# A hybrid decoder trunk on one core: the mixer's weight scan with three buffers, the gate product on GpSimd, and layer 1's FFN groups and small sums in another order

## The chip, the cores and the metric

The kernel runs on one core of a Trainium2 chip. The metric is the time of one execution on the device in microseconds (us); a kernel is given by the median of its runs. The engines work at the same time, each through its own list of instructions in order: TensorE (PE in the profile; PEld is its weight load), VectorE (DVE), ScalarE (ACT), GpSimd (POOL) and SyncE (SP, which issues DMA transfers here). An instruction can wait for another engine's result; everything behind it on its own engine then waits too. L12 is line 12 of the kernel.

## What is computed

Two layers on 1024 tokens of width 1024, float32 in and out. Layer 0 mixes by differential attention and a Mamba-2 state-space part, layer 1 by a Conformer convolution module; each is followed by a gated FFN with a causal convolution of width 3 over the tokens.

```python
def conformer_conv(h, ...):                      # layer 1's mixer
    u = h @ pw1_w + pw1_b
    u = u[..., :1024] * sigmoid(u[..., 1024:])
    u = causal_dwconv(u, dw_w, dw_b)             # width 31
    u = silu(layer_norm(u, ln_w, ln_b))
    return u @ pw2_w + pw2_b

def conv_ffn(h, up_w, conv_w, conv_b, down_w):
    u = causal_dwconv(h @ up_w, conv_w, conv_b)  # width 3
    gate, val = u[..., :2816], u[..., 2816:]
    return (silu(gate) * val) @ down_w

def reference(x, ...):
    for i in range(2):
        if i == 0:
            x = x + hybrid_mixer(rms_norm(x, mix_norm_w), ...)
        else:
            x = x + conformer_conv(rms_norm(x, conf_norm_w), ...)
        x = x + conv_ffn(rms_norm(x, ffn_norm_w[i]), ...)
    return x
```

## The kernel before

**Tiles.** Tokens lie along the free dimension, in two halves of 512 (`h` = 0, 1). A product of the trunk is `gemm`: for each of 8 blocks of 128 channels three matmuls of 128x512 float16, since both sides are split into a high and a low part; so 24 matmuls, all on L239. The FFN's 2816 columns are 22 tiles ("pairs", a gate tile and a value tile). They stand in groups: one of 6 pairs that is computed for both halves with its weights loaded once (`BOTH`; A in layer 0, E in layer 1), and B and C of 8 pairs each, computed for one half at a time (`HALVES`; B[0], B[1] and so on). `ups` makes a group's pairs, `close` scales and splits its gated values to float16 (L935 on ScalarE, L936 on VectorE), `down` multiplies by the down weights and adds into x (L1063).

**Weights.** `loads` brings a weight tile by SyncE's queue into one of three raw buffers. ScalarE casts it (L94, or L98), and the low part comes from GpSimd (L95, L96; for the "pool" groups and the conv weights) or VectorE (L99). Pool groups are those of the half whose conv runs at the time: layer 0's B, C of half 1, layer 1's of half 0.

**Powers.** The scale of a weight matrix is a power of two, found from the sum of squares over the whole matrix. `scan` makes it in the background: it loads a piece by ScalarE's own queue, squares and sums it there (L147). In the mixer it goes over layer 0's up weights, 88 pieces of 256 KB, with one buffer, a step each time that `mix` has made a step of the mixer's own work. `root` and `total` turn sums into a power: a reduction (L132), one small matmul that sums over partitions (L110), and small VectorE operations (L112, L120, L125, L126). `powers(1)` does so for layer 1's up weights and its norm weight.

**Norms.** `rms`: token sums of squares by small matmuls (L903), an inverse root by VectorE (L248 to L254), a broadcast by matmul into PSUM (L259), then for each block a product on VectorE (L920), a cast on ScalarE (L932) and a subtraction on VectorE (L933). `ln` does it twice: the mean (L903, L259; subtracted in L1144, squared on ScalarE, summed in L1150), then the variance (L903, L259), then L1158, a SiLU, and the split.

**Order.** Each engine's order follows from the order in which the program records its instructions, with priorities (`high_priority`) that let weight loads and evictions go ahead. Generators yield where other work may be put between. `along` runs the conv (`p1`, `ln`: 30 multiply-adds of 128x512 a block on VectorE, L1123) beside FFN pairs of the other half. `weave` runs a norm beside products. In layer 1: conv of half 1 with B[0] and C[0] beside it; then `p2(1)`, the conv module's second product; then the norm of half 1 woven with what is left of B[0] and C[0] (`f`); then B[1], C[1] and last E for both halves.

**The gate.** For a pair, `conv3` evicts the product with the width-3 convolution (ScalarE L945 or L947, VectorE L951), ScalarE applies the SiLU (L981), `gate` multiplies the two (L961 on VectorE) and ScalarE squares the result for its power (L962). These tiles are `a`, with six buffers.

Of the kernel before, what the change touches and what calls it, by code (L numbers as in the profile page):

```python
# [20 lines left out]
P = 128  # L21
# [19 lines left out]
MIXER = {"raw": 2, "whl": 4, "g": 10, "scan": 1, "sums": 1}  # L41
PIECE = 4, 8
TRUNK = {"raw": 3, "w": 4, "g": 20, "sv": 1, "hf": 2, "scan": 2, "gm": 4, "gs": 4, "sums": 5}


class Net:
# [91 lines left out]
    def scan(self, name, srcs, depth):  # L138
# [5 lines left out]
        for i, src in enumerate(srcs + [None] * depth):  # L144
# [3 lines left out]
            if src is not None:  # L148
                t = self.T("scan", [P, PIECE[depth - 1], P])[:, 0:src.shape[1]]
                nc.scalar.dma_start(t, src)  # L150
                todo.append((i, t))
# [10 lines left out]
    def scan_up(self, l, depth=2):  # L162
        ups = [self.I["ffn_up_w"][l, j] for j in range(2 * NP)]
        return self.scan(f"up{l}", self.pieces(PIECE[depth - 1], *ups), depth)

    def scan_down(self, l, depth=2):
        return self.scan(f"down{l}", self.pieces(PIECE[depth - 1], *[self.I["ffn_down_w"][l, c] for c in range(KT)]), depth)

    def scan_conf(self, depth=2):
        yield from self.scan("pw1", self.pieces(PIECE[depth - 1], *[self.I["conf_pw1_w"][j] for j in range(2 * KT)]), depth)  # L170
        yield from self.scan("pw2", self.pieces(PIECE[depth - 1], *[self.I["conf_pw2_w"][c] for c in range(KT)]), depth)

# [647 lines left out]
    def wout(self, K, att):  # L820
# [18 lines left out]
        self.mix(att, 3, wg, 3)  # L839
        self.wout_b(w, 1)  # L840

    def mix(self, a, na, b, nb):

        for _ in merged(a, na, b, nb):
            next(self.bg, None)

    def mixer(self):
        self.heads, self.attT = {}, {}
        with self.phase("mixer", MIXER), self.psum("p1", mm=2, t=6):
            self.bg = self.scan_up(0, 1)  # L850
# [5 lines left out]
            self.mix(self.ssd(), 20, chain(self.zgate(), self.qkv(1)), 16)  # L856
# [100 lines left out]
    def gate(self, G, i, h, ga, va):  # L957
# [3 lines left out]
        nc.vector.tensor_mul(g[:], va[:], ga[:])  # L961
# [26 lines left out]
    def first_pairs(self, G):  # L988
# [3 lines left out]
        js = (G.k0, NP + G.k0, G.k0 + 1, NP + G.k0 + 1)  # L992
        ws = [self.loads(self.I["ffn_up_w"][G.l, k], KT, self.pows[f"up{G.l}"][0]) for k in js]
# [201 lines left out]
    def trunk_tail(self):  # L1195
# [3 lines left out]
        A.have = 2  # L1199
# [12 lines left out]
        f = chain(f, self.beside(chain(self.ups(C[1], (B[1], None)), self.finish(B[1], C[1], self.stat_add)), bg))  # L1212
# [7 lines left out]
        self.powers(1)  # L1220
# [182 lines left out]
```

## Time and profile before

| | |
|---|---|
| median of 3 runs | 2316.85 us (2313.42 to 2317.26) |
| the profiled execution | 2315.64 us, its span 2313.9 us |
| TensorE busy | 2211.3 us (96% of the span) |
| VectorE busy | 1581.0 us (68%) |
| ScalarE busy | 1386.1 us (60%) |
| GpSimd busy | 414.1 us (18%) |
| mean granted TensorE clock | 0.977 of full speed |

The span is what the trace covers; the profiled execution's own time is 1.7 us longer. An engine's share is a mean over stretches with different limits: the mixer takes the time up to about 615 us, the trunk the rest. A busy TensorE is not always at full speed: the granted clock says how fast it ran.

### The profile page before, as it was taken

Reading aid. Unit: us, or ns where it says so; the run is one execution under the profiler, and the core shown is the slowest. Engines: PE = TensorE matmul, PEld = TensorE weight load, DVE = VectorE, ACT = ScalarE, POOL = GpSimd, SP = SyncE. Lnnn points to the kernel's source line nnn. Section 1 sums busy time; section 2 is a strip of 40 time slices with the busy share of each in tenths; the row PEclk is TensorE's granted clock in tenths of the full one; section 3 lists DMA queues with packets and bytes.
Section 4 is the critical chain, followed back from the end, with each engine's and each line's share of the span. In section 5 each row is a group of like instructions: output and inputs, shape, how many; then the busy total and the mean of one; then the engine's idle time right before and its main releaser. Section 6 shows DMA issues by size and latency. Waiting matters only on the chain. (4 is left out here: it accounts for less than half of the span.)

```text
span 2313.9 us, 29051 instructions
## 1 busy us (share of the span) xinstructions
PE 2211.3 (96%) x10767; PEld 1232.9 (53%) x10767; DVE 1581.0 (68%) x2951; ACT 1386.1 (60%) x2197; POOL 414.1 (18%) x304
## 2 busy tenths in 40 slices
PE   8999988889899999999999998999996999999999
PEld 7778987777544444444444443444443444444444
DVE  6886566776755546455889998599996446556452
ACT  7775467753566667686677756577866534444330
POOL 0000000033000000012544444245441400000000
PEclk9999989999899999999999999999997999999999
DMA  6222223221356576755233332233331333331122
GB/s 185 91 90 86 71 92 99 82 81 50 114 184 197 187 243 204 253 191 166 85 98 102 108 94 72 73 110 106 95 100 55 100 100 102 107 101 56 46 74 82
DMA packets 87886, 262.09 MB, mean 113 GB/s; under 512 B 12864, under 2 KB 15552, under 8 KB 87744
## 3 DMA queue, kind: packets, MB, share of 16 engines
q1 hardware_dynamic: 58368, 178.44, 24.7%
q10 hardware_dynamic: 29376, 81.80, 11.1%
q8 instruction: 84, 1.38, 0.2%
q14 instruction: 58, 0.48, 0.1%
HBM read 256.01 MB, written 4.19 MB: 112 GB/s over the span
## 5 line engine op out<-in xcount | busy, mean ns | idle before, releaser
L239 PEld LDWEIGHTS <-w 128*128 128x128 f16 x7488 | 736.6, 99 | 901.3 <-issue 31.3
L239 PE MATMUL pmm<-h,w 128*128 128x512 f16 x5376 | 1178.2, 382 | 14.3 <-DVE h L933 5.7
L239 PE MATMUL pmm<-g,w 128*128 128x512 f16 x2112 | 461.4, 380 | 0.0
L96 POOL TENSOR_TENSOR w<-raw,w 128x1024 f16<-128x1024 f32 x144 | 310.3, 2156 | 592.8 <-ACT raw L95 585.6
L951 DVE SCALAR_TENSOR_TENSOR a<-pmm,c_ffn_conv_w,a 128x511 f32<-128x511 f32 (+1 forms) x352 | 262.0, 745 | 167.9 <-ACT a L945 164.3
L1123 DVE SCALAR_TENSOR_TENSOR pt<-u,c_conf_dw_w,pt 128x512 f32<-128x512 f32 x480 | 337.1, 747 | 6.5 <-ACT pt L1120 4.1
L147 ACT ACTIVATE scan<-scan 128x1024 f32<-128x1024 f32 (+2 forms) x204 | 173.4, 850 | 120.7 <-DMA scan<-ffn_up_w 98.0
L239 PE MATMUL pmm<-h,whl 128*128 128x512 f32 x912 | 232.9, 406 | 0.0
L239 PEld LDWEIGHTS pmm<-h,whl 128*128 128x128 f32 x912 | 169.3, 191 | 37.1
L1063 DVE SCALAR_TENSOR_TENSOR x<-pmm,gs,x 128x512 f32<-128x512 f32 x96 | 71.9, 749 | 156.5 <-PE pmm L239 156.5
L429 PE MATMUL pmm<-whl,h 128*128 128x384 f32 (+1 forms) x672 | 139.1, 355 | 14.3 <-ACT h L230 10.0
L945 ACT ACTIVATE a<-pmm,c_ffn_conv_b,c_ffn_conv_w 128x512 f32<-128x512 f32 x112 | 86.6, 773 | 90.0 <-PE pmm L239 88.3
L99 DVE SCALAR_TENSOR_TENSOR w<-raw,c_su_up,w 128x1024 f16<-128x1024 f32 x88 | 112.6, 1281 | 27.1 <-ACT w L98 26.3
L429 PEld LDWEIGHTS pmm<-whl,h 128*128 128x128 f32 x672 | 119.1, 192 | 18.7 <-ACT h L230 10.3
L962 ACT ACTIVATE a<-g 128x512 f32<-128x512 f32 x88 | 55.3, 628 | 119.8 <-DVE g L961 119.5
L98 ACT ACTIVATE w<-raw,c_su_up 128x1024 f16<-128x1024 f32 x88 | 100.0, 1138 | 38.9 <-PE pmm L239 31.0
L98 ACT ACTIVATE w<-raw,c_su_down 128x1024 f16<-128x1024 f32 (+1 forms) x48 | 51.3, 1070 | 66.7 <-PE pmm L239 65.7
L981 ACT ACTIVATE a<-a 128x512 f32<-128x512 f32 x84 | 52.6, 626 | 55.3 <-DVE a L951 43.2
L94 ACT ACTIVATE w<-raw,c_su_up 128x1024 f16<-128x1024 f32 x64 | 72.7, 1138 | 8.9 <-PE pmm L239 8.8
L947 ACT ACTIVATE a<-pmm,c_ffn_conv_b,c_ffn_conv_w 128x510 f32<-128x510 f32 x64 | 49.4, 774 | 47.3 <-PE pmm L239 47.3
L961 DVE TENSOR_TENSOR g<-a,a 128x512 f32<-128x512 f32 x88 | 75.3, 856 | 1.9 <-ACT a L981 0.9
L95 ACT ACTIVATE raw<-raw,c_su_up 128x1024 f32<-128x1024 f32 x64 | 73.1, 1144 | 3.9
(316 smaller groups left out, 2272.8 us busy)
## 6 DMA issues: line engine op xcount, KB each, us to landing
raw<-ffn_up_w SPq DMA_DIRECT2D x152, 512.0 KB, 3.7
raw<-ffn_down_w SPq DMA_DIRECT2D x64, 512.0 KB, 3.5
raw<-conf_pw_w SPq DMA_DIRECT2D x48, 512.0 KB, 3.6
scan<-ffn_up_w ACTq DMA_DIRECT2D x88, 256.0 KB, 2.6
scan<-ffn_up_w ACTq DMA_DIRECT2D x44, 512.0 KB, 4.7
scan<-ffn_down_w ACTq DMA_DIRECT2D x32, 512.0 KB, 4.1
scan<-conf_pw_w ACTq DMA_DIRECT2D x24, 512.0 KB, 4.3
raw<-w_out SPq DMA_DIRECT2D x16, 448.0 KB, 3.3
```

Source lines behind the costliest of these rows:

```text
L94: nc.scalar.activation(w[:, 0], raw[:], AF.Copy, scale=scale)
L95: nc.scalar.activation(raw[:], raw[:], AF.Copy, scale=scale)
L96: nc.gpsimd.tensor_sub(w[:, 1], raw[:], w[:, 0])
L98: nc.scalar.activation(w[:, 0], raw[:], AF.Copy, scale=scale)
L99: nc.vector.scalar_tensor_tensor(w[:, 1].rearrange("p k m -> p (k m)"), raw.rearrange("p k m -> p (k m)"), scale, w[:, 0].rearrange("p k m ...
L147: nc.scalar.activation(t, t, AF.Square, accum_out=sums[:, k:k + 1])
L239: self.nc.tensor.matmul(ps, w[:, a, k, :], h[:, b, :], start=n == 0, stop=n == last)
L429: nc.tensor.matmul(ps[:, 0:n], h[:, a, tc_], ws[k // 2][:, b, k % 2, :], start=i == 0, stop=i == 3 * KT - 1)
L945: nc.scalar.activation(a[:], ps[:], AF.Identity, bias=b, scale=w[:, 2:3])
L951: nc.vector.scalar_tensor_tensor(a[:, d:], ps[:, 0:HALF - d], wd, a[:, d:], ALU.mult, ALU.add)
L961: nc.vector.tensor_mul(g[:], va[:], ga[:])
L1123: nc.vector.scalar_tensor_tensor(y[:], u[:, k:k + HALF], w[:, k:k + 1], y[:], ALU.mult, ALU.add)
```

## The change

The mixer's scan gets three buffers and a depth of three (three pieces in flight), and `mix` takes two of its steps a turn in the state-space part; buffer `g` goes from 10 to 9 for it. The gate product of pool groups moves from VectorE to GpSimd. `powers(1)` moves from the norm of half 1 into the FFN work beside the conv of half 0. In layer 1 group E takes the first six pairs and B, C the others; the rest of `f` runs ahead of `p2(1)`; behind `p2(1)` come `first_pairs(E)`, E's other pairs, then B[1] with E's down product inside, C[1], and the down products of B[1] and C[1].

```diff
-MIXER = {"raw": 2, "whl": 4, "g": 10, "scan": 1, "sums": 1}
-PIECE = 4, 8
-TRUNK = {"raw": 3, "w": 4, "g": 20, "sv": 1, "hf": 2, "scan": 2, ...
+MIXER = {"raw": 2, "whl": 4, "g": 9, "scan": 3, "sums": 1}
+PIECE = {2: 8, 3: 4}
+TRUNK = {"raw": 3, "w": 4, "g": 20, "sv": 1, "hf": 3, "scan": 2, ...
@@ wout
-        self.mix(att, 3, wg, 3)
+        self.mix(att, 3, islice(wg, 1), 1)
+        run(wg)
@@ mix
-    def mix(self, a, na, b, nb):
+    def mix(self, a, na, b, nb, scan=1):
         for _ in merged(a, na, b, nb):
-            next(self.bg, None)
+            steps(self.bg, scan)
@@ mixer
-            self.bg = self.scan_up(0, 1)
+            self.bg = self.scan_up(0, 3)
...
-            self.mix(self.ssd(), 20, chain(self.zgate(), self.qkv(1)), 16)
+            self.mix(self.ssd(), 20, chain(self.zgate(), self.qkv(1)), 16, 2)
@@ gate
-        nc.vector.tensor_mul(g[:], va[:], ga[:])
+        (nc.gpsimd if G.pool else nc.vector).tensor_mul(g[:], va[:], ga[:])
@@ trunk_tail, layer 0
-        f = chain(f, self.beside(chain(self.ups(C[1], (B[1], None)), self.finish(B[1], C[1], self.stat_add)), bg))
+        f = chain(f, self.beside(chain(self.ups(C[1], (B[1], None)), self.call(self.powers, 1),
+                                       self.finish(B[1], C[1], self.stat_add)), bg))
...
         self.weave(f, 10, self.rms(1, self.cnw))
-        self.powers(1)
         run(f)
@@ trunk_tail, layer 1
-        B, C = self.halves(1, 0)
-        E = Group(1, HALVES[0] + HALVES[1], BOTH, (0, 1))
+        B, C = self.halves(1, BOTH)
+        E = Group(1, 0, BOTH, (0, 1))
         f = chain(self.ups(B[0]), self.ups(C[0], (B[0], None), "down1"), self.finish(B[0], C[0]))
-        along(chain(p1, self.ln(1)), 206, f, 210)
+        along(chain(p1, self.ln(1)), 206, f, 215)
+        run(f)
         run(self.p2(1))
-        ahead(f, 5.2)
-        self.weave(f, 10, self.rms(1, self.fnw[:, 1, :]))
+        run(self.first_pairs(E))
+        run(self.ups(E))
+        run(self.ups(B[1], (E, lambda c, h: h or self.store(c, h))))
+        run(self.ups(C[1], (B[1], None)))
+        f = self.down(B[1])
+        ahead(f, 2 * 5.2)
+        self.close(C[1])
         run(f)
-        run(self.ups(B[1]))
-        run(self.ups(C[1], (B[1],)))
-        e = self.ups(E)
-        ahead(e, 4 * 5.2)
-        self.close(C[1])
-        run(e)
-        f = self.down(C[1])
-        ahead(f, 3 * 5.2)
-        self.close(E)
-        run(f)
-        run(self.down(E, self.store))
+        run(self.down(C[1], self.store))
```

The numbers of matmuls stay the same. From line 146 on the changed kernel's lines stand one or two further down (L903 becomes L904, L933 becomes L934; L259 and L110 stay).

**TensorE at the end of the conv of half 1.** Before, this is its order from the last product of the FFN's down tile `pmm_2342` on: the second token sum of `ln` (on `rb`), its broadcast (L259), and the first products of `p2`, which read the normalised `h`.

```order
L239 MATMUL pmm_2342_14946<-g_2216_13933,w_2341_14942 128x512
L903 MATMUL pt_2333_14896<-c_ones_71,rb_2306_14763 128x1 [waits DVE_49,PE_49]
L903 MATMUL pt_2333_14896<-c_ones_71,rb_2306_14763 128x1 x3
L259 MATMUL pt_2337_14917<-c_ident_66,tiny_2334_14901 128x128 [waits DVE_49]
L259 MATMUL pt_2337_14917<-c_ident_66,tiny_2334_14901 128x128 x3
L239 LDWEIGHTS w_2346_15000
L239 MATMUL pmm_2347_15004<-h_2338_14924,w_2346_15000 128x512 [waits Activation_49]
```

In the changed kernel the same three (L904, L259, the first product on `h_2338`) stand among products on the FFN's `g`, with their waits:

```order
L239 MATMUL pmm_2341_14933<-g_2214_13924,w_2340_14929 128x512
L904 MATMUL pt_2333_14896<-c_ones_71,rb_2306_14763 128x1 [waits DVE_49]
L904 MATMUL pt_2333_14896<-c_ones_71,rb_2306_14763 128x1 x3
L239 LDWEIGHTS w_2340_14929
L239 MATMUL pmm_2341_14933<-g_2215_13927,w_2340_14929 128x512
...
L239 MATMUL pmm_2350_15028<-g_2211_13915,w_2349_15024 128x512
L259 MATMUL pt_2337_14917<-c_ident_66,tiny_2334_14901 128x128 [waits DVE_49,PE_49]
L259 MATMUL pt_2337_14917<-c_ident_66,tiny_2334_14901 128x128 x3
L239 LDWEIGHTS w_2349_15024
...
L239 MATMUL pmm_2383_15388<-h_2338_14924,w_2382_15384 128x512 [waits DVE_49]
```

Between the first broadcast of `ln` (not shown) and L904 stood 14 products and now stand 51; between L904 and L259 none and now 39; between L259 and the first product on `h_2338` none and now 255.

**VectorE at the end of the norm of half 0 ahead of the first conv.** Before, the gate product L961 stands ahead of the last subtraction of the norm (L933, into `h_1669`), for which the conv's first products wait:

```order
L948 SCALAR_TENSOR_TENSOR a_1680_9758<-pmm_1679_9733,c_ffn_conv_w_594,hf_1532_8842 128x2 [waits Activation_49]
L951 SCALAR_TENSOR_TENSOR a_1674_9716<-pmm_1673_9691,c_ffn_conv_w_594,a_1674_9716 128x510 [waits DVE_49]
L951 SCALAR_TENSOR_TENSOR a_1680_9758<-pmm_1679_9733,c_ffn_conv_w_594,a_1680_9758 128x510 [waits DVE_49]
L961 TENSOR_TENSOR g_1675_9721<-a_1674_9716,a_1656_9635 128x512 [waits DVE_49]
L933 TENSOR_TENSOR h_1669_9678<-a_1670_9681,h_1669_9678 128x512 [waits Activation_49]
L1099 SCALAR_TENSOR_TENSOR u_1689_9830<-pmm_1688_9805,c_conf_pw1_b_600,a_1685_9797 128x512 [waits PE_49,Activation_49]
```

In the changed kernel the gate is gone from this queue:

```order
L949 SCALAR_TENSOR_TENSOR a_1680_9758<-pmm_1679_9733,c_ffn_conv_w_594,hf_1532_8842 128x2 [waits Activation_49]
L952 SCALAR_TENSOR_TENSOR a_1674_9716<-pmm_1673_9691,c_ffn_conv_w_594,a_1674_9716 128x510 [waits DVE_49]
L952 SCALAR_TENSOR_TENSOR a_1680_9758<-pmm_1679_9733,c_ffn_conv_w_594,a_1680_9758 128x510 [waits DVE_49]
L934 TENSOR_TENSOR h_1669_9678<-a_1670_9681,h_1669_9678 128x512 [waits Activation_49]
L1101 SCALAR_TENSOR_TENSOR u_1689_9830<-pmm_1688_9805,c_conf_pw1_b_600,a_1685_9797 128x512 [waits PE_49,Activation_49]
```

It stands on GpSimd now (L962), where it waits for both `a` tiles and behind whatever weight subtraction is ahead of it.

## Rows read from the trace of the kernel before

**Rows 1.** The page, part 1: busy us, share of the span, instructions.
```profile
PE 2211.3 (96%) x10767; PEld 1232.9 (53%) x10767; DVE 1581.0 (68%) x2951; ACT 1386.1 (60%) x2197; POOL 414.1 (18%) x304
```

**Rows 2.** The page, part 4: the chain that ended last, by engine.
```profile
PE 32%; DVE 6%; ACT 0%; issue 0%; DMA 0%; POOL 0%; ACTq 0%; DVEq 0%; POOLq 0%
```

**Rows 3.** Windows: window, us, busy us and instructions by engine, granted clock, DMA share, GB/s.
```profile
1438.00:1452.00 14.00, 6.92 (x26) 2.89 (x24) 10.50 (x26) 5.42 (x7) 6.95 (x6) 0.76 0.20 68
1500.00:1550.00 50.00, 50.00 (x234) 22.64 (x232) 48.70 (x78) 38.67 (x45) 24.07 (x12) 1.00 0.34 106
1740.00:1775.00 35.00, 15.49 (x63) 8.28 (x62) 28.72 (x59) 22.22 (x34) 2.36 (x2) 0.66 0.10 31
```

**Rows 4.** Timeline, 1740 to 1767 us: start, duration, engine, line, idle before.
```profile
1740.21 2.48 DVE L1144 TENSOR_TENSOR h<-h,pt 128x512 f32<-128x512 f32 x4 [1.18 <-PE pt L259]
...
1749.95 0.73 DVE L1063 SCALAR_TENSOR_TENSOR x<-pmm,gs,x 128x512 f32<-128x512 f32 x1
...
1751.39 0.69 DVE L1150 TENSOR_TENSOR rb<-rb,a 128x512 f32<-128x512 f32 x1
...
1752.23 1.83 PE L903 MATMUL pt<-c_ones,rb 128*128 128x1 f32 x8 [8.89 <-DVE tiny L120]
...
1755.25 5.38 DVE L936 SCALAR_TENSOR_TENSOR g<-g,gs,g 128x512 f16<-128x512 f32 x8
...
1761.74 2.08 PE L259 MATMUL pt<-c_ident,tiny 128*128 128x128 f32 x8 [7.68 <-DVE tiny L254]
...
1766.76 1.01 PE L239 MATMUL pmm<-h,w 128*128 128x512 f16 x2 [2.94 <-ACT h L935]
```

**Rows 5.** Timeline at the two L110, 1436 to 1450 and 1623 to 1631 us.
```profile
1442.42 3.20 DVE L933 TENSOR_TENSOR h<-a,h 128x512 f16<-128x512 f32 x2
...
1446.17 0.56 PE L110 MATMUL pt<-tiny,c_ones 128*128 128x1 f32 x2 [7.08 <-DVE tiny L132]
...
1629.50 0.38 PE L110 MATMUL pt<-tiny,c_ones 128*128 128x1 f32 x2 [1.76 <-DVE tiny L1043]
```

**Rows 6.** Timeline, 1114 to 1123 us.
```profile
1118.50 2.12 POOL L96 TENSOR_TENSOR w<-raw,w 128x1024 f16<-128x1024 f32 x1 [1.86 <-ACT raw L95]
1118.89 2.29 DVE L961 TENSOR_TENSOR g<-a,a 128x512 f32<-128x512 f32 x1
...
1121.83 1.44 PE L239 MATMUL pmm<-h,w 128*128 128x512 f16 x3 [4.45 <-DVE h L933]
```

**Rows 7.** Windows in the mixer, columns as above.
```profile
150.00:300.00 150.00, 150.00 (x915) 134.76 (x914) 97.19 (x192) 78.87 (x167) 2.27 (x5) 1.00 0.25 78
300.00:425.00 125.00, 107.48 (x653) 95.45 (x651) 84.67 (x249) 90.98 (x239) 2.08 (x4) 0.90 0.28 86
```

**Rows 8.** Timeline of TensorE, 618 to 664 us, layer 0's first pairs.
```profile
625.95 38.37 PE L239 MATMUL pmm<-h,w 128*128 128x512 f16 x177
```

**Rows 9.** L961 alone; groups of GpSimd; waits of ScalarE: us, times, longest.
```profile
L961 DVE TENSOR_TENSOR g<-a,a x88: 674/692/2366, 629.6 to 2209.7; 128x512 f32<-128x512 f32 x88
...
L96 POOL TENSOR_TENSOR w<-raw,w 128x1024 f16<-128x1024 f32 x144 | 310.3, 2156 | 592.8 <-ACT raw L95 585.6 <-issue 4.6 <-PE pmm L239 1.4
...
L1132 POOL TENSOR_TENSOR sv<-sv,h 128x512 f32<-128x512 f32 x10 | 12.8, 1277 | 2.2 <-ACT h L1127 2.0
...
ACT a L962 <- DVE g L961: 119.5, 68, 2.8
```

**Rows 10.** Groups of ScalarE, 300 to 425 us: busy, mean ns, idle before.
```profile
L147 ACT ACTIVATE scan<-scan 128x512 f32<-128x512 f32 x28 | 17.6, 629 | 8.7 <-DMA scan<-ffn_up_w 8.5
```

**Rows 11.** Waits of TensorE, 300 to 425 us: us in total, times, longest.
```profile
PE pt L764 <- DVE a L762: 6.2, 2, 4.6
PE pt L534 <- DVE x L523: 4.7, 2, 2.6
```

**Rows 12.** Window 4 to 8 us; DMA issues of the scan: KB, us to landing.
```profile
4.00:8.00 4.00, 0.00 (x0) 0.00 (x0) 0.05 (x1) 1.64 (x4) 0.00 (x0) 1.00 1.10 358
...
scan<-ffn_up_w ACTq DMA_DIRECT2D x88, 256.0 KB, 2.6
```

More of the change, by code (lines that the diff above doesn't have):

```diff
@@ L40 @@
 KEPT = {"h": 16, "x": 8, "u": 2, "a": 6, "rb": 2, "tiny": 7, "eh": 1}
-MIXER = {"raw": 2, "whl": 4, "g": 10, "scan": 1, "sums": 1}
-PIECE = 4, 8
-TRUNK = {"raw": 3, "w": 4, "g": 20, "sv": 1, "hf": 2, "scan": 2, "gm": 4, "gs": 4, "sums": 5}
+MIXER = {"raw": 2, "whl": 4, "g": 9, "scan": 3, "sums": 1}
+PIECE = {2: 8, 3: 4}
+TRUNK = {"raw": 3, "w": 4, "g": 20, "sv": 1, "hf": 3, "scan": 2, "gm": 4, "gs": 4, "sums": 5}
 class Net:
@@ L148, in scan @@
             if src is not None:
-                t = self.T("scan", [P, PIECE[depth - 1], P])[:, 0:src.shape[1]]
+                t = self.T("scan", [P, PIECE[depth], P])[:, 0:src.shape[1]]
                 nc.scalar.dma_start(t, src)
@@ L163, in scan_up @@
         ups = [self.I["ffn_up_w"][l, j] for j in range(2 * NP)]
-        return self.scan(f"up{l}", self.pieces(PIECE[depth - 1], *ups), depth)
+        return self.scan(f"up{l}", self.pieces(PIECE[depth], *ups), depth)
     def scan_down(self, l, depth=2):
-        return self.scan(f"down{l}", self.pieces(PIECE[depth - 1], *[self.I["ffn_down_w"][l, c] for c in range(KT)]), depth)
+        return self.scan(f"down{l}", self.pieces(PIECE[depth], *[self.I["ffn_down_w"][l, c] for c in range(KT)]), depth)
     def scan_conf(self, depth=2):
-        yield from self.scan("pw1", self.pieces(PIECE[depth - 1], *[self.I["conf_pw1_w"][j] for j in range(2 * KT)]), depth)
-        yield from self.scan("pw2", self.pieces(PIECE[depth - 1], *[self.I["conf_pw2_w"][c] for c in range(KT)]), depth)
+        yield from self.scan("pw1", self.pieces(PIECE[depth], *[self.I["conf_pw1_w"][j] for j in range(2 * KT)]), depth)
+        yield from self.scan("pw2", self.pieces(PIECE[depth], *[self.I["conf_pw2_w"][c] for c in range(KT)]), depth)
     def squares(self, v, n):
@@ L992, in first_pairs @@
         js = (G.k0, NP + G.k0, G.k0 + 1, NP + G.k0 + 1)
+        G.have = 2
         ws = [self.loads(self.I["ffn_up_w"][G.l, k], KT, self.pows[f"up{G.l}"][0]) for k in js]
@@ L1198, in trunk_tail @@
         A = Group(0, 0, BOTH, (0, 1))
-        A.have = 2
         B, C = self.halves(0, BOTH)
@@ L1224, in trunk_tail, with call @@
         self.weave(p1, 3, self.rms(0, self.fnw[:, 1, :]))
[L1225 to L1226 removed]
+        B, C = self.halves(1, BOTH)
+        E = Group(1, 0, BOTH, (0, 1))
         f = chain(self.ups(B[0]), self.ups(C[0], (B[0], None), "down1"), self.finish(B[0], C[0]))
[L1228 removed]
+        along(chain(p1, self.ln(1)), 206, f, 215)
+        run(f)
         run(self.p2(1))
[L1230 to L1243 removed]
+        run(self.first_pairs(E))
[5 more added lines that the diff above has]
+        self.close(C[1])
+        run(f)
+        run(self.down(C[1], self.store))
+    def call(self, f, *a):
+        f(*a)
+        return
+        yield
     def beside(self, f, bg):
```

## The prediction

> **What bounds the kernel now.** I read the page first. TensorE is busy 2211.3 of 2313.9 us and VectorE 68% of them [rows 1], and the chain that ended last is a third TensorE and 6% VectorE, with nothing of size from DMA [rows 2]. So a gain can only come from the 102.6 us in which TensorE stands still, and from the half-speed stretches behind the longer of those stands. Inside the trunk's long stretches nothing is to be had: from 1500 to 1550 us TensorE is busy 50.00 of 50 with 234 matmuls, 0.214 us each at granted clock 1.00, while VectorE too is busy 48.7 [rows 3]. That 0.214 us is the price of one 512-column product below; one gemm of 24 is 5.1 us.
>
> Next the waits of TensorE, in order of time, at the places that the change touches: 8.89 us ahead of L903 and 7.68 us ahead of L259 [rows 4], 7.08 us ahead of L110 [rows 5], each released by a small VectorE operation that ends a chain, and 4.45 us ahead of a product [rows 6]. Last the mixer, where 300 to 425 us has 107.48 us of TensorE at mean clock 0.90, while the stretch ahead of it is full [rows 7].
>
> **The layer-1 changeover between conv and second product (1740 to 1775 us).** From 1740 to 1775 us TensorE has 63 matmul records at mean clock 0.66 [rows 3]. 43 are 512-column products, 43 x 0.214 = 9.2 us; the 20 small ones are worth about 2.4 us at full clock (the eight of L903 and eight of L259 took 1.83 and 2.08 us at half clock [rows 4]). So 35 - 11.6 = 23.4 us are lost. The reason is in the rows: behind L259 at 1740 only 14 products stand, VectorE then needs until 1752.1 for the eight L1144 and L1150, TensorE takes L903 at 1752.23, VectorE first splits eight tiles of the FFN group (L936, 5.38 us) and only then finishes the root, TensorE takes L259 at 1761.74 and waits again until 1766.76 for the first normalised tile. The changed order puts the rest of FFN group B, C there: 51 products (10.9 us) between first L259 and second token sum, 39 (8.4 us) between that and second L259, 255 (54.6 us) before the first product of p2. The vector chain itself is not shorter: 1740.21 to 1752.08, 11.9 us, and one more eviction like L1063's 0.73 us falls into it; from 1752.23 to the end of the root at 1761.7 it is 9.5 us, some 0.9 less at full clock. So about 1.5 us of stall stay at the first place and about 0.5 at the second, none at the third, and I add 1 us for slower clock. 23.4 - 3 = **-20**. Bounds: -23.4 if nothing stays; -12 if the chains grow by half, 6 and 4 us more, each stall then with its half-speed tail.
>
> The products that were to cover the next norm are thereby used up. That norm now lies over the first pairs of group E: two gemms of half 0 stand ahead of its broadcast and two behind it. Layer 0's group A is written in the same way, and there TensorE ran 38.37 us on without a gap behind L259 [rows 8]. I take 0, with +5 (one gemm) as the bound.
>
> **Layer 1's powers, moved.** At 1446.17 TensorE has stood 7.08 us at L110; VectorE reached the small operations only when the last L933 of half 1 was done (1442.42 + 3.20 us for two) [rows 5]. From 1438 to 1452 us the mean clock is 0.76 [rows 3], which adds about 2 us for nine products at half clock. Both go, -9, if the products that come next have what they need: hn of half 1 is complete at 1445.6; when the stand began, at 1439.1, 50 products that don't need it still stood ahead in TensorE's order, 10.7 us, to 1449.8. The two L110 now stand among FFN products during the conv of half 0. They wait there for a vector queue full of L1123; the nearest row is L110 at 1629.50, the same kind of sum inside the other conv, which cost 1.76 us [rows 5]. I take +1 (0 to +4).
>
> **The gate product on GpSimd (32 of 88).** VectorE is spared at least 32 x 0.69 = 22 us [rows 9], but in stretches where TensorE is full: worth nothing there. Only one place has TensorE waiting behind a gate: at 1118.89 L961 takes 2.29 us instead of 0.69, beside a GpSimd subtraction that began at 1118.50, and the last L933 of the norm stands behind it; TensorE waits 4.45 us [rows 6]. With that gate gone from VectorE's queue: **-2**. On GpSimd a product of this size has no row; the nearest is L1132, also two 128x512 float32 inputs, 1277 ns [rows 9]. It must queue behind subtractions of 2156 ns [rows 9], so a gate is done up to 3 us later. That is covered by six buffers of a (a gate is needed once in 10 us) and by four buffers of weights; uncovered it is the third rival. The Trainium skill ("SBUF — State Buffer", section "SBUF: two separate sides") says that GpSimd and a VectorE operation with two SBUF inputs exclude each other for a whole instruction. The stretched L961 agrees. By that rule a gate on GpSimd still takes its 1.3 us from VectorE's two-input operations, which speaks against the move; the sum by it would lose no more than those 2 us.
>
> **The mixer's scan.** ScalarE squares 28 pieces from 300 to 425 us: 17.6 us of work and 8.7 us of standing, nearly all for their transfers [rows 10]. In the change all 88 are over by the end of the state-space part, whose 150 us are full on TensorE with ScalarE busy 78.87 of 150 [rows 7]; those 28 squares fit there. What TensorE gets back is not those 26 us: its waits in that stretch are 125 - 107.5 = 17.5 us, the two largest for vector results (L762, L523) [rows 11]. L762 adds squares that ScalarE makes, so a part of such a wait is ScalarE being behind; how much no row tells. The bounds are 0, and the 26 us that ScalarE is spared. I take two fifths of 17.5 us, -7, and -2 for the clock, which follows these waits (0.90 of 125 us). Against it stands the start: three 256 KB pieces instead of one go out before x and the first weights, while the DMA engines move 358 GB/s [rows 12]: 512 KB more is +1.4 us on TensorE's first matmul. Also a square now and then just ahead of an exponential in the state-space part, 0 to +3, taken as 1. Sum -7 - 2 + 1.4 + 1 = **-6.6** (+4.4 to -23.6).
>
> The order of the last projection's products in the mixer and the tail are the same work as before: 0.
>
> **Sum:** -20 - 9 + 1 - 2 - 6.6 = -36.6. Against the profiled run's 2315.64 us this gives 2279.0. The median of the runs shown is 2316.85, 1.2 above the profiled one, so the predicted median is **2280 us**.
>
> **Rivals.**
> 1. The mixer gives nothing (the waits there are VectorE's own): 2280 + 7 = 2287. For it: the largest waits name VectorE [rows 11]. It may also give its far bound, 17 us more: 2263.
> 2. The stalls of the changeover only move: E's norm waits for half 1 (+5), the moved L110 cost +4 (3 more than taken), and the ln chain keeps 11 instead of 3 us (+8): about 2280 + 16 = 2296. For it: VectorE's chains are as long as before. Against it: layer 0's first pairs [rows 8].
> 3. It ends slower: GpSimd's gates. Each L962 on ScalarE waits for its gate (119.5 us in 68 cases even now [rows 9]), and the weight casts of the next tiles are queued behind it; GpSimd takes gate and weight subtractions in order. If a gate holds TensorE up by more than 36.6 / 32 = 1.1 us each, the gain is gone; at the 3 us from above, 2280 + 96 = 2376 us. Against it: GpSimd is busy 24.07 of 50 us in the conv [rows 3] and stood waiting for ScalarE 585.6 us [rows 9]; a gate of 1.3 us each 10 us adds some 6 us to 50.
>
> **How the numbers follow.** My forecast (2272 to 2286) 0.60; mixer without effect or a little worse (2286 to 2292) 0.13; far gains (below 2272) 0.09; rival 2 (2292 to 2302) 0.10; rival 3 weak (2302 to 2312) 0.01, even (2312 to 2321) 0.02, strong (above) 0.05. What the runs of this kernel tell from no change is about 0.2%, 4.6 us. Faster by over 0.2%: 0.93; within: 0.02; slower: 0.05. The range takes in the mixer's far bound and nearly all of rival 2, and leaves out what is above: 2263 to 2300.
>
> **What would show it.** L904's second token sum and second L259 in the changeover with under 2 us idle ahead of each, and clock 1.00 there; no L110 with over 2 us; TensorE 4 to 10 us more in 300 to 425 us; no L147 behind 300 us; L962 on GpSimd near 1.3 us with TensorE still at 234 matmuls in 50 us of the conv. I am wrong if TensorE's waits in the conv name GpSimd or ScalarE's weight casts, if the first product on hn of half 1 in group E waits by over 2 us, or if the first matmul comes later than 11 us.

## The result and the profile after

The changed kernel takes 2301.06 us (median of 6 runs, 2295.18 to 2305.38), the kernel before beside it 2313.89 (6 runs): a ratio of 0.994, 95% interval 0.9921 to 0.9958. It is faster, by 12.8 us; 2280 was predicted, 2263 to 2300 its range. The profiled run was the fastest, 2295.18 us with a span of 2293.4, 20.5 below the span before. It lies 5.9 us below the median of its own kernel. So I read first where those 20.5 us are, and then what the other runs have that this one has not.

The page after, parts 1 and 4, answers to [rows 1, 2]:

```profile
PE 2209.9 (96%) x10767; PEld 1228.2 (54%) x10767; DVE 1549.3 (68%) x2923; ACT 1376.2 (60%) x2191; POOL 452.2 (20%) x336
...
PE 24%; DVE 1%; ACT 0%; issue 0%
```

TensorE's busy time is the same within 1.4 us; what went is standing. VectorE has 32 us less, GpSimd 38 more. VectorE is nearly gone from the chain (6% before): the large waits for its small sums no longer end last.

The start times of the same TensorE instruction in both traces, each with the same products behind it, show where time came and went, in us:

| point | before | after | difference |
|---|---|---|---|
| first matmul | 9.4 | 10.4 | +1.1 |
| L259 of layer 0's first FFN norm (end of the mixer) | 625.1 | 619.0 | -6.1 |
| L110 of B[1]'s close, in the first conv | 1185.9 | 1179.9 | -6.0 |
| L110 of C[1]'s close, behind the place of the moved powers | 1325.9 | 1327.1 | +1.2 |
| L259 of the norm of half 1 in `p2(0)`, behind `ln(0)` and ahead of the old place of the powers | 1422.8 | 1428.9 | +6.1 |
| token sum of the FFN norm of half 0 in layer 1, behind the old place of the powers | 1469.4 | 1466.0 | -3.4 |
| first token sum of `ln(1)` | 1719.5 | 1713.9 | -5.6 |
| last instruction | 2313.9 | 2293.4 | -20.5 |

The mixer's end lies 6.1 us earlier, with 6.6 forecast; further down it turns out that this trace is a lucky one there. The old place of the powers gave 9.5 us, with 9 forecast. What is missing was lost at the new place of the powers (+7.2 for +1), in `ln(0)` and `p2(0)` (+4.9 for 0), ahead of the first conv, where the gate's 2 us did not come (+0.1), and in the changeover, which gave 14.9 of the 20 us. The second conv gave 2.2 us that are in no term: TensorE's waits there are not shorter (5.7 us for 4.7), but the clock is higher behind the second of its small sums (1.00 from 1617.67 to 1640 us; before 0.90 from 1622.27 to 1640). The windows of the powers and the changeover, with those of the mixer, columns as in [rows 3, 7]:

```profile
300.00:425.00 125.00, 111.51 (x708) 99.28 (x707) 93.81 (x286) 77.47 (x199) 2.07 (x4) 0.95 0.09 27
425.00:500.00 75.00, 60.91 (x327) 48.78 (x327) 58.90 (x128) 44.03 (x97) 17.80 (x12) 0.90 0.31 107
1296.00:1312.00 16.00, 12.66 (x47) 5.25 (x46) 12.80 (x35) 7.98 (x11) 7.06 (x4) 0.79 0.40 108
1720.00:1760.00 40.00, 35.00 (x165) 17.25 (x164) 31.77 (x61) 25.86 (x35) 12.09 (x6) 0.91 0.27 79
```

From 1720 to 1760 us, the changeover, 5 of 40 us of standing and a clock of 0.91 are left; before, TensorE stood 19.5 of 35 us, at 0.66 [rows 3]. From 1296 to 1312 us there is now 0.79 where the conv ran at 1.00. In the mixer 300 to 425 us has 4 us more of TensorE at 0.95, and 425 to 500 us a clock of 0.90, where it was 0.93 before.

**The changeover.** Timeline of the changed kernel, columns as in [rows 4]:

```profile
1724.70 0.38 PE L904 MATMUL pt<-c_ones,h 128*128 128x1 f32 x2 [2.56 <-ACT h L1129]
...
1728.03 2.48 DVE L1146 TENSOR_TENSOR h<-h,pt 128x512 f32<-128x512 f32 x4 [1.34 <-PE pt L259]
...
1735.77 2.03 DVE L1152 TENSOR_TENSOR rb<-rb,a 128x512 f32<-128x512 f32 x1
...
1739.14 2.13 POOL L96 TENSOR_TENSOR w<-raw,w 128x1024 f16<-128x1024 f32 x1 [1.90 <-ACT raw L95]
...
1739.82 1.99 DVE L1152 TENSOR_TENSOR rb<-rb,a 128x512 f32<-128x512 f32 x1
...
1742.67 1.05 PE L904 MATMUL pt<-c_ones,rb 128*128 128x1 f32 x8 [2.00 <-DVE rb L1152]
...
1749.89 2.13 POOL L96 TENSOR_TENSOR w<-raw,w 128x1024 f16<-128x1024 f32 x1 [8.62 <-ACT raw L95]
1750.01 2.02 DVE L252 TENSOR_TENSOR tiny<-tiny 128x4 f32<-128x4 f32 x1
...
1754.28 1.13 PE L259 MATMUL pt<-c_ident,tiny 128*128 128x128 f32 x8 [0.44 <-DVE tiny L254]
```

The third wait of 2.94 us is gone, as forecast. Both of VectorE's chains are longer than before: from the first L1146 to the second token sum 14.6 us (12.0 in [rows 4]), and from there to the second L259 11.6 us (9.5 in [rows 4]). In the second chain a VectorE operation on 4 numbers a partition (L252) takes 2.02 us: it starts when GpSimd is 0.12 us into a weight subtraction and ends as that ends. In [rows 4] the same operations are not among the rows because none took more than 0.17 us. In the first chain two additions (L1152) take 2.03 and 1.99 us, where 0.68 is usual; the one at 1739.82 ends 0.54 us behind a subtraction. GpSimd is there because of the moved products: their down weights belong to a pool group. The rest of the longer chains is mostly three more evictions (L1065, some 0.7 us each) and 1.6 us in which VectorE waits for products.

One such meeting was there before the change too, between the rows of [rows 4]:

```profile
1746.16 2.12 POOL L96 TENSOR_TENSOR w<-raw,w 128x1024 f16<-128x1024 f32 x1 [5.92 <-ACT raw L95]
1746.21 2.62 DVE L1150 TENSOR_TENSOR rb<-rb,a 128x512 f32<-128x512 f32 x1
```

So 1.9 of the 11.9 us that the prediction gives the first chain were a stretched addition.

**The gate.** Timeline of the changed kernel in the second conv:

```profile
1683.64 8.58 PE L239 MATMUL pmm<-h,w 128*128 128x512 f16 x39
...
1685.85 0.74 DVE L952 SCALAR_TENSOR_TENSOR a<-pmm,c_ffn_conv_w,a 128x510 f32<-128x510 f32 x1
1686.11 2.12 POOL L96 TENSOR_TENSOR w<-raw,w 128x1024 f16<-128x1024 f32 x1 [3.06 <-ACT raw L95]
...
1688.19 1.27 POOL L962 TENSOR_TENSOR g<-a,a 128x512 f32<-128x512 f32 x1
...
1689.50 0.63 ACT L963 ACTIVATE a<-g 128x512 f32<-128x512 f32 x1 [3.47 <-POOL g L962]
...
1690.13 0.76 ACT L946 ACTIVATE a<-pmm,c_ffn_conv_b,c_ffn_conv_w 128x512 f32<-128x512 f32 x1
...
1690.92 0.75 DVE L952 SCALAR_TENSOR_TENSOR a<-pmm,c_ffn_conv_w,a 128x511 f32<-128x511 f32 x1 [1.63 <-ACT a L946]
```

VectorE ends the value tile at 1686.59; GpSimd has just begun a weight subtraction, the gate runs from 1688.19, and ScalarE, which squares it, has stood 3.47 us. Behind that square stands the eviction of the next product (L946), and VectorE waits 1.63 us for it, with the conv's multiply-adds behind. TensorE runs through all this without a gap (39 products in 8.58 us). ScalarE's waits for the gate in the whole second conv (1480 to 1740 us: us, times, longest):

```profile
ACT a L963 <- POOL g L962: 44.2, 16, 3.5
```

Before, the same waits were 15.0 us. At the one place where the forecast had a gain, ahead of the first conv, TensorE still waits 3.32 us (4.45 in [rows 6]):

```profile
1112.87 1.26 POOL L962 TENSOR_TENSOR g<-a,a 128x512 f32<-128x512 f32 x1 [1.76 <-DVE a L952]
1113.36 1.32 DVE L934 TENSOR_TENSOR h<-a,h 128x512 f16<-128x512 f32 x1
...
1114.74 3.57 PE L239 MATMUL pmm<-h,w 128*128 128x512 f16 x8 [3.32 <-DVE h L934]
```

The gate is gone from VectorE's queue, but it runs on GpSimd at that moment, and the last subtraction of the norm (L934) takes 1.32 us beside it in place of 0.68.

**The moved powers.** TensorE of the changed kernel at the two small sums, answers to [rows 5]:

```profile
1294.38 0.28 PE L110 MATMUL pt<-tiny,c_ones 128*128 128x1 f32 x2
1294.52 3.83 PE L239 MATMUL pmm<-g,w 128*128 128x512 f16 x17
1301.69 0.59 PE L110 MATMUL pt<-tiny,c_ones 128*128 128x1 f32 x2 [3.34 <-DVE tiny L132]
```

17 products stand between them, 3.8 us; the second waits 3.34 us for VectorE.

**The mixer.** Its two largest waits of TensorE from 300 to 500 us, answers to [rows 11]:

```profile
PE pt L570 <- DVE u L567: 6.8, 3, 5.1
PE pt L461 <- DVE g L458: 6.7, 1, 6.7
```

The waits at L764 and L551 are gone; those at L570 and L461, which were 1.3 and 4.6 us over the same stretch before, have grown to 13.5 together. Part of the gain is given back to VectorE's chains behind 425 us.

### The profile page after: what moved, and what is told of

It reads as the page before. It is cut to its first block, busy times and chain, and to the rows that moved or that the text cites. A ratio compares the mean times of both kernels' runs of the same rounds, so it can differ in the third digit from the quotient of the medians.

```text
span 2293.4 us, 28980 instructions
## 1 busy us (share of the span) xinstructions
PE 2209.9 (96%) x10767; PEld 1228.2 (54%) x10767; DVE 1549.3 (68%) x2923; ACT 1376.2 (60%) x2191; POOL 452.2 (20%) x336
## 5 line engine op out<-in xcount | busy, mean ns | idle before, releaser
L239 PE MATMUL pmm<-h,w 128*128 128x512 f16 x5376 | 1173.9, 381 | 10.9 <-DVE h L934 5.0
L239 PE MATMUL pmm<-g,w 128*128 128x512 f16 x2112 | 468.9, 384 | 0.0
L1065 DVE SCALAR_TENSOR_TENSOR x<-pmm,gs,x 128x512 f32<-128x512 f32 x96 | 71.9, 749 | 174.1 <-PE pmm L239 174.0
L946 ACT ACTIVATE a<-pmm,c_ffn_conv_b,c_ffn_conv_w 128x512 f32<-128x512 f32 x112 | 86.4, 771 | 76.4 <-PE pmm L239 74.3
L94 ACT ACTIVATE w<-raw,c_su_pw 128x1024 f16<-128x1024 f32 x48 | 54.7, 1140 | 37.2 <-PE pmm L239 33.6
```

Source lines behind the costliest of these rows:

```text
L94: nc.scalar.activation(w[:, 0], raw[:], AF.Copy, scale=scale)
L239: self.nc.tensor.matmul(ps, w[:, a, k, :], h[:, b, :], start=n == 0, stop=n == last)
L946: nc.scalar.activation(a[:], ps[:], AF.Identity, bias=b, scale=w[:, 2:3])
L1065: self.nc.vector.scalar_tensor_tensor(self.xs(c, h), ps[:], G.u[h], self.xs(c, h), ALU.mult, ALU.add)
```

## The experiments

Each was timed against the kernel before on its own chip; ratios are to it.

**The changed kernel again.** No edit.

> The changed kernel once more, as the measure for the three beside it. Its runs lay between 2295 and 2305 us, and the one profiled (2295.2 us) was the fastest. If the spread is one of the chip's state, this profile shows the same waits of TensorE as the first (69 us in sum) and runs again scatter over some 10 us; if it belongs to a wait that falls out one way or the other, a profile of a slower run has another wait that is longer.

Measured: 2300.1 us (2297.25 to 2303.97), 0.9939 (0.9927 to 0.9951). This time the profiled run was a long one, 2303.97 us. It is 3.2 us behind the first at the end of the mixer, and 5.8 more are lost from the first token sum of `ln(1)` on; between the two it agrees with the first within 0.3 us at every point of the table. Its changeover:

```profile
1755.27 2.13 POOL L96 TENSOR_TENSOR w<-raw,w 128x1024 f16<-128x1024 f32 x1 [9.75 <-ACT raw L95]
1755.39 2.02 DVE L252 TENSOR_TENSOR tiny<-tiny 128x4 f32<-128x4 f32 x1
...
1758.64 2.12 POOL L96 TENSOR_TENSOR w<-raw,w 128x1024 f16<-128x1024 f32 x1 [1.24 <-ACT raw L95]
1758.78 2.00 DVE L254 SCALAR_TENSOR_TENSOR tiny<-tiny,tiny 128x4 f32<-128x4 f32 x1
...
1761.51 2.05 PE L259 MATMUL pt<-c_ident,tiny 128*128 128x128 f32 x8 [3.43 <-DVE tiny L254]
```

Here two operations of the root stand for 2 us each beside GpSimd, L252 and L254, and TensorE waits 3.43 us and then runs at half speed. In the first trace only one did, and the wait was 0.44 us. So one part of the scatter is whether a 0.16 us operation falls onto a subtraction. Two more traces below have the same order there (the powers at the old place, and the norm's power apart): in both, two operations of the root are stretched, and TensorE waits 3.04 us. The 3 us in the mixer I could not put down to one wait.

**The gate back on VectorE.**

```diff
-        (nc.gpsimd if G.pool else nc.vector).tensor_mul(g[:], va[:], ga[:])
+        nc.vector.tensor_mul(g[:], va[:], ga[:])
```

> The changed kernel with the gate product back on VectorE for all groups. Theory 1, the gate on GpSimd eats part of the gain (ScalarE's square waits for it, 29.1 us in the first conv against 10.3 before, with the next eviction and weight cast queued behind it, so the conv chain on VectorE ends no earlier): 4 to 8 us faster than the changed kernel, the waits of TensorE at the ends of both convs shorter. Theory 2, the gate is harmless and the order alone costs: within 2 us of the changed kernel, or up to 4 us slower because VectorE has 22 us more to do.

Measured: 2292.24 us, 0.9909 (0.9895 to 0.9923), 7.9 us faster than the changed kernel on the same chip. ScalarE's wait for the gate in the second conv falls from 44.2 to 20.0 us:

```profile
ACT a L963 <- DVE g L962: 20.0, 12, 2.8
```

And the moved powers cost nothing any more. TensorE at the same two sums:

```profile
1298.24 0.28 PE L110 MATMUL pt<-tiny,c_ones 128*128 128x1 f32 x2
1298.38 7.93 PE L239 MATMUL pmm<-g,w 128*128 128x512 f16 x36
1306.22 0.38 PE L110 MATMUL pt<-tiny,c_ones 128*128 128x1 f32 x2
```

36 products stand between them now, 7.9 us, and there is no wait. The order of TensorE is fixed when the program is built, and with the gate on GpSimd it puts the second sum 17 products behind the first. That it does so because VectorE's queue then looks emptier to it is my reading and not shown.

The gate's place changes the order elsewhere too. Against the second trace of the changed kernel TensorE needs 6.2 us less here at the powers; 8.0 less from the first token sum of `ln(1)` on, where 85 products stand ahead of that sum's other parts in place of 37, and then 83 and 12 ahead of the next two steps in place of 51 and 39; and 4.9 more at the close of B[0] in the second conv, where it waits 5.08 us behind 18 products in place of 2.41 behind 10. In the two long stretches of the convs, where ScalarE stands for the gates, it is only 0.4 and 0.6 us. So the gate costs by the cover that the new order takes away, and ScalarE's waits as such hardly reach TensorE.

**The powers back at the old place.**

```diff
-        ...self.ups(C[1], (B[1], None)), self.call(self.powers, 1), self.finish(...)
+        ...self.ups(C[1], (B[1], None)), self.finish(...)
...
         self.weave(f, 10, self.rms(1, self.cnw))
+        self.powers(1)
```

> The changed kernel with layer 1's powers back in the norm of half 1. Theory 1, the new place costs 6.8 us (3.3 us of wait at the second small sum, the rest half-speed clock behind it) and the old one 9.5: 2 to 4 us slower than the changed kernel. Rival, what is lost in the first conv comes from the gates and not from the moved sums, as the prediction had it (+1): 8 us slower.

Measured: 2298.75 us, 0.9929 (0.9917 to 0.9942), 1.4 us faster than the changed kernel. Beside the gate on GpSimd the move is worth nothing within the noise, which is less than either theory had.

**The norm's power apart.**

```diff
 def powers(self, l):
         self.rooted(f"up{l}")
-        self.norm_powers(f"norm{l}", self.fnw[:, l, :])
+        if l == 0:
+            self.norm_powers(f"norm{l}", self.fnw[:, l, :])
 def conf_powers(self):
         self.norm_powers("cnorm", self.cnw[:])
+        self.norm_powers("norm1", self.fnw[:, 1, :])
```

> The changed kernel with the power of layer 1's norm weight, which needs no scan, made with the conv's powers, so that only one small sum, whose result nobody awaits soon, is left in the first conv. Theory 1, the wait is the chain between two sums with 17 products of cover: the 3.3 us wait and its half-speed tail go, 4 to 7 us faster than the changed kernel. Rival, TensorE then only comes earlier to the end of the conv, whose chain on VectorE ends when it ends: 0 to 2 us faster, and the token sum behind the conv waits longer by what was saved.

Measured: 2292.36 us, 0.9905 (0.989 to 0.992), 7.7 us faster than the changed kernel, a little more than the first theory had: the wait between the two sums was the cost (6.6 us less there in its trace), and its going is not eaten up at the end of the conv. The sum that went waits 2.27 us at its new place, among the conv's powers.

**The mixer's scan alone, on the kernel before.** Its edit is the change's diff for MIXER, PIECE, `wout`, `mix` and `mixer`.

> The kernel before with only the mixer's scan changed (three buffers, depth three, two steps a turn in the state-space part, over by its end). Theory, the mixer's part is worth what the two traces show at the first norm of the trunk: 5 to 7 us faster than before, the first matmul 1.1 us later. Rival, the run-to-run scatter of 3 us in the mixer covers it: under 3 us.

Measured: 2310.7 us, 0.9986 (0.9977 to 0.9995): 3 us, with bounds of 1 and 5. In its profile the end of the mixer lies 3.2 us earlier than before. The gain is there, at half of what I took, at the edge between theory and rival.

**Layer 1's order alone, on the kernel before.** Its edit is the last piece of the change's diff, with three buffers `hf`.

> The kernel before with only layer 1's order changed (rest of the FFN ahead of the second conv product, group E with its first pairs behind it). Theory, what stays of the 23 us there is small VectorE operations that stand for 2 us each behind GpSimd's weight subtractions, which the moved products bring with them: 10 to 15 us faster than before, with one to three operations of 0.16 us stretched to 2 us between 1730 and 1765 us. Rival, as predicted only the plain chains stay: 20 us faster.

Measured: 2302.66 us, 0.9956 (0.9943 to 0.9968), about 10 us. That is in the theory's range, and half of the forecast, but not by the theory's sum. In its profile 17.0 us are gained from the first token sum of `ln(1)` on. What is stretched there is no 0.16 us operation but two additions of the first chain (L1151, 2.27 and 2.46 us), and TensorE waits 3.51 us at the second token sum. And 3.8 us are given back earlier, at the close of B[0] in the second conv: 18 products stand between its two small sums in place of 24, and TensorE waits 5.08 us in place of 1.76. That comes of the weight 215, which is in the same piece of the diff.

**Both edits.** The gate on VectorE and the norm's power apart.

> The changed kernel with the gate back on VectorE and layer 1's norm power made with the conv's powers. If the two gains are of different places they add: 2285 us, 15 us faster than the changed kernel. Rival, both take the same stall at the end of the first conv, so that the second adds only what lies elsewhere: 2288 to 2291 us.

Measured: 2290.38 us, 0.9902 (0.9889 to 0.9916), 9.7 us faster than the changed kernel by medians of two chips. The rival: both edits take away the same wait at the powers. By the ratios this kernel and the one with the norm's power apart and the gate on GpSimd are the same (0.9902 and 0.9905): where the powers are out of the way, the gate's place shows no cost beyond the noise. The changeover's stall remains in it:

```profile
1750.06 4.67 POOL L96 TENSOR_TENSOR w<-raw,w 128x1024 f16<-128x1024 f32 x2 [8.22 <-ACT raw L95]
...
1752.81 2.46 DVE L1154 TENSOR_TENSOR rb<-rb,a 128x512 f32<-128x512 f32 x1 [0.91 <-ACT a L1153]
...
1755.33 1.87 PE L906 MATMUL pt<-c_ones,rb 128*128 128x1 f32 x8 [3.51 <-DVE rb L1154]
```

**Both edits, without GpSimd in the changeover.**

```diff
-  ..., "down1"), self.finish(B[0], C[0]))
+  ..., "down1"), self.call(self.nopool, B[0], C[0]), self.finish(B[0], C[0]))
+    def nopool(self, *gs):
+        for G in gs:
+            G.pool = False
```

> The kernel with both edits, and with the weights of the down products that fill the changeover of layer 1 split on VectorE in place of GpSimd (16 subtractions fewer on GpSimd, 16 of 1.28 us more on VectorE). Theory, the chains of the norm there are stretched because GpSimd's subtractions shut out VectorE's operations with two inputs in SBUF: no stretched operation is left there, TensorE's waits ahead of the second token sum and the second broadcast under 1 us each, 3 to 5 us faster than the kernel with both edits. Rival, the 1.28 us operations lie in the same chains and cost as much: within 2 us.

Measured: 2285.62 us, 0.9881 (0.9866 to 0.9896), 4.8 us faster than with both edits on the same chip, as the theory has it. The window of the changeover, columns as before:

```profile
1735.00:1770.00 35.00, 34.89 (x180) 17.84 (x179) 30.85 (x63) 15.66 (x23) 0.00 (x0) 1.00 0.24 74
```

GpSimd 0.00, TensorE 34.89 of 35 us at clock 1.00. No operation of the chains is stretched, and TensorE waits nowhere in them. This is what the prediction had for the place, and it took away GpSimd's part of the moved products to get it. But TensorE's order is another here too, 69 and 34 products ahead of the two steps in place of 83 and 12, so that the 4.8 us are not the price of the meetings alone.

**The gate alone, on the kernel before.** The diff of the change's gate.

> The kernel before with only the gate product of pool groups on GpSimd. Theory, it costs by itself, because ScalarE's square waits for it and holds up evictions: 2 to 6 us slower than before, ScalarE's waits for the gate in both convs near 30 us. Rival 1, the prediction's: 2 us faster. Rival 2, it costs only together with the moved sums, whose order it tightens (17 products of cover in place of 36): within 2 us of before.

Measured: 2315.87 us, 1.0012 (1.0003 to 1.0021), 2.7 us slower, with bounds of 0.7 and 4.9: the theory's range, but the second rival (within 2 us) is not excluded. The profiled run is a short one, with a span 1.1 us below that before, so its trace does not show where the 2.7 us are. ScalarE's waits for the gate in the second conv, and a wait of TensorE at the end of the first conv (1340 to 1480 us) that the kernel before does not have:

```profile
ACT a L962 <- POOL g L961: 44.7, 16, 3.8
```

```profile
PE pt L903 <- ACT h L1127: 3.0, 1, 3.0
```

The wait at the second token sum behind it is shorter for that, 1.4 us in place of 3.0.

**The powers alone, on the kernel before.** The diff of the change's powers.

> The kernel before with only layer 1's powers moved into the first conv; with the gate on VectorE 36 products stand between its two small sums. Theory, the move is worth what was predicted where nothing else tightens it: 6 to 9 us faster than before, under 2 us of wait at its sums. Rival, the sums hold TensorE up in the conv whatever the gate does, as in the changed kernel where the move gave nothing: within 3 us of before.

Measured: 2306.39 us, 0.9968 (0.9956 to 0.998), 7 us by the ratio: the forecast's -8. In its trace the old place gives 9.5 us and the new one costs 0.5. Without the gate's move the step was right.

**A close's sum made early.** On the kernel with both edits and without GpSimd in the changeover, which waits 5.06 us at the second small sum of the second conv (its timeline):

```profile
1611.89 0.28 PE L110 MATMUL pt<-tiny,c_ones 128*128 128x1 f32 x2
...
1621.13 0.59 PE L110 MATMUL pt<-tiny,c_ones 128*128 128x1 f32 x2 [5.06 <-DVE tiny L1047]
```

```diff
 def ups(...):
...
+            early = pending is not None and pending[1:] == (None,)   # no down product inside
             if pending is not None and i == G.have + 1:
...
-                self.close(pending[0])
+                if early:
+                    F = pending[0]
+                    for h in F.hs:
+                        self.nc.vector.tensor_reduce(F.gm[h][:, 15:16], F.gm[h][:, 0:F.n], AX.X, ALU.add)
...
+                else:
+                    self.close(pending[0])
+            if early and i == G.have + 2:
+                self.close(pending[0])
```

`close` then takes the sum that is made here. The edit acts on all three groups that are closed in this way, two of them elsewhere.

> The kernel with both edits and without GpSimd in layer 1's changeover, and with the sum for a group's close, which TensorE waited 5.1 us for in the second conv, made on VectorE one pair ahead of the small matmul that needs it. Theory, that wait and its half-speed tail go: 4 to 7 us faster than the kernel without this edit (2285.6), about 2280 us. Rival, TensorE then waits for the end of the conv instead: 0 to 2 us faster.

Measured: 2283.01 us, 0.9866 (0.9853 to 0.9878), 2.6 us faster by medians of two chips, between the two ranges. The wait is gone, but TensorE stands at the end of the conv instead, as the rival has it (waits, 1480 to 1800 us):

```profile
PE pt L906 <- POOL sv L1148: 6.7, 1, 6.7
```

So nothing is gained at this place. In the trace the gain lies in `ln(0)` and `p2(0)`, a stretch that varies from kernel to kernel, as said below.

**The FFN's weight against the conv back at 210.**

```diff
-        along(chain(p1, self.ln(1)), 206, f, 215)
+        along(chain(p1, self.ln(1)), 206, f, 210)
```

> The kernel with both edits and without GpSimd in the changeover, with the FFN's weight against the conv put back from 215 to 210. By its order 24 products stand between the two small sums of the second conv in place of 18, as in the kernel before. Theory, the 5.1 us wait at the second of them (1.8 in the kernel before) came with 215: it falls to about 2 us, and the kernel is 3 to 5 us faster than 2285.6. Rival, the time goes to the end of the conv: within 2 us.

Measured: 2279.44 us (2277.77 to 2282.72), 0.9853 (0.9829 to 0.9876). TensorE at the same two sums:

```profile
1610.13 0.28 PE L110 MATMUL pt<-tiny,c_ones 128*128 128x1 f32 x2
1610.27 5.34 PE L241 MATMUL pmm<-h,w 128*128 128x512 f16 x24
1617.37 0.38 PE L110 MATMUL pt<-tiny,c_ones 128*128 128x1 f32 x2 [1.76 <-DVE tiny L1047]
```

24 products in place of 18, and 1.76 us as in [rows 5]. The wait is the theory's; the gain, 6.2 us by medians of two chips, is more than its 3 to 5. In the changeover 51 products stand again ahead of the second token sum, as in the changed kernel, and GpSimd is still out of it:

```profile
1735.51 11.17 PE L241 MATMUL pmm<-g,w 128*128 128x512 f16 x51
1735.57 2.48 DVE L1148 TENSOR_TENSOR h<-h,pt 128x512 f32<-128x512 f32 x4 [0.35 <-PE pt L261]
...
1746.52 0.99 PE L906 MATMUL pt<-c_ones,rb 128*128 128x1 f32 x8
```

The first chain, with two evictions in it, now takes 10.95 us in place of the changed kernel's 14.6, and TensorE does not wait. This is the fastest kernel of the study, 33.7 us below the kernel before on its chip. That is near what was forecast for the change, but it took the gate back on VectorE, GpSimd out of the changeover and the weight back at 210.

## Why the prediction was wrong

The sign and the places were right. The sum was off by 21 us, 16 of them in the first trace, which itself lies 5.9 us below the median of its runs; these steps failed.

**The changeover, -20 forecast; -14.9 in the first trace, -9.0 in the second, -17.0 in the trace of the order alone.** The failed step is "The vector chain itself is not shorter: 1740.21 to 1752.08, 11.9 us [...] So about 1.5 us of stall stay at the first place and about 0.5 at the second". With the terms of that step the chains are 12.6 and 8.6 us; they came out at 14.6 and 11.6. I took their length from a stretch in which GpSimd was busy 2.36 of 35 us [rows 3], one stretched addition included, and laid products over it whose weights GpSimd splits. That the stalls of the first trace are still near the forecast (2.00 and 0.44 us) is luck: the products over them were slow as well (12.9 and 10.3 us for the forecast's 10.9 and 8.4), at a clock of 0.91. In the second trace the second stall is 3.43 us.

That GpSimd stretches the operations is shown by the traces of the changed kernel, of both edits and of the order alone, in which they end with a subtraction or some 0.55 us behind it, and by the kernels without those subtractions, in which none is stretched. The Trainium skill has the rule ("SBUF — State Buffer", section "SBUF: two separate sides"): whichever of GpSimd and a VectorE operation with two SBUF inputs starts first keeps the other out until it is done. The runs agree, with 2.0 us for an operation of 0.16. I had weighed that rule for the gate and not for the products that I counted as cover. How much of the missing 5 to 11 us the meetings cost is not measured by itself, since each edit there also changes TensorE's order.

A further wait of 2.56 us, ahead of the first token sum of `ln(1)`, was not in the forecast. There 37 products stand between the first part of that sum and the others, where 80 stood before; all five traces with the gate on GpSimd have the wait, and none with the gate on VectorE.

**The gate, -2 forecast, 2.7 us slower alone, 8 us slower together with the rest.** Two steps failed. The first is "With that gate gone from VectorE's queue: **-2**": the wait fell only from 4.45 to 3.32 us, since the gate on GpSimd stretches the same subtraction. The second is that the price was looked for in the late gate alone, "covered by six buffers of a (a gate is needed once in 10 us) and by four buffers of weights". The gates did come late, and the buffers did not keep ScalarE from standing, since it takes its list in order (44.2 us); but TensorE was covered there within about half a us in each of the two long stretches. What had no term is that the move changes TensorE's built order, and with it the cover at the powers and in the changeover, as the kernel with the gate back shows. The price of a gate was right (1.27 us; GpSimd and VectorE beside each other in the changed kernel, ns min, median, max):

```profile
L962 DVE TENSOR_TENSOR g<-a,a x56: 682/691/694, 623.5 to 2210.3; 128x512 f32<-128x512 f32 x56
L962 POOL TENSOR_TENSOR g<-a,a x32: 1262/1268/2177, 1018.6 to 1719.9; 128x512 f32<-128x512 f32 x32
```

The third rival saw a loss, but by another way, through ScalarE's queue. 8 us over 32 gates is 0.25 us of TensorE each, below the 1.1 us from which it decides, so the change stays faster.

**The powers, -9 and +1 forecast; -9.5 and +7.2 in the first trace, -7 alone, nothing in the changed kernel.** The old place is right. The failed step is "the nearest row is L110 at 1629.50 [...] which cost 1.76 us": I took the price from a place with 24 products between the two sums, and did not count the 17 that the changed order puts there, though it could be read in that order. TensorE waits 3.34 us and then runs at a lower clock (0.79 from 1296 to 1312 us). That it is the gate's move which takes the cover away is shown by the same change with the gate on VectorE and by the powers alone (36 products, no wait in either).

**The mixer, -6.6 forecast, -6.1 and -2.9 in two traces of the changed kernel, -3 alone.** The start was right (+1.1 for +1.4). The failed step is the size, "I take two fifths of 17.5 us, -7". Over all traces, L259 of layer 0's first FFN norm starts at 618.99 to 623.05 us in the ten traces with the changed mixer and at 623.07 to 626.59 in the four with the old one; the means lie 3.3 us apart. So the -6.1 of the first trace was luck, and the gain is half of what I took. I stopped at 425 us, and waits for VectorE behind it grew.

**First pairs of E, 0 forecast:** right. Behind its L259 TensorE runs on without a gap in the changed kernel too.

**`ln(0)` and `p2(0)`, not in the forecast, +4.9 and +4.8 in the two traces.** The cause stays open. From C[1]'s close to the L259 of half 1's norm TensorE takes 102.5 us in the changed kernel and 97.6 before. But it is 99.3 in two kernels that change nothing there (the mixer alone and layer 1's order alone), 103.6 with the gate back on VectorE, and 97.2 with the gate on GpSimd and the norm's power apart. So neither the gate nor the powers explain it by themselves.

Singly the four parts are worth -3, -10, -7 and +3 us, -18 in sum by the ratios, and 14 together. The 4 us between are within what the intervals of five ratios leave open; that gate and powers take cover from one another is shown by the traces, not by this sum.

## What to carry to other kernels

Products that are moved over a wait bring their operands' work with them: before counting them as cover, ask which engine prepares their weights, and whether that engine shares something with the chain that is to be covered. An operation that goes to an idle engine is not judged by the load of the engine that it leaves: ask what it stretches there, and read the new order of the engine that bounds the kernel, which such a move can change far from its own place. Count the products between two dependent steps in that order; a price from a row holds only for the same count. And a trace is one run: the first of these was 5.9 us better than the median, and two of its terms looked right by luck.

## What was not expected of the hardware

An operation on 128x4 numbers in VectorE took 2.0 us beside a GpSimd subtraction of 2.12 us, some twelve times its 0.16; in proportion the smallest operations of a chain lose most. It works the other way as well: a gate of 1.26 us moved to GpSimd made a subtraction of 0.68 us on VectorE take 1.32. And the same kernel's runs scatter by 10 us (2295.18 to 2305.38): of the 8.8 us between the two that were traced, 5.8 lie in and behind the changeover, where one such operation of the root is hit in the one and two in the other.
